# A two-layer gated-linear-attention decoder step on eight cores: 256-token pairs, one mixed last tile, cast weight loads during the other phase, sample states in phase 2, decay kept in the state

## The chip, the cores and the metric

One Trainium2 chip, all eight cores, one program on each: a core has one prompt sequence of 2048 positions and 16 sample sequences of 4 tokens, and no core talks to another. The metric is device time in microseconds (us) of the slowest core. Cores 0 to 3 are one die, 4 to 7 the other. In some executions the cores of one die show a lower granted TensorE clock and take some per cent longer (in one of before, 1661.4 us, cores 0 to 3 had a mean clock of 0.80 to 0.82 and took 1611 to 1660 us, cores 4 to 7 had 0.92 to 0.93 and took 1494 to 1519); such an execution is called slow, and only fast ones are compared.

## The reference

Each of two layers does this for every token (cut to what matters here; `gla_scan` is the recurrence over tokens, `pool_mix` trailing means over 2, 4, 8 and 16 positions):

```python
xn = rmsnorm(h, norm_g)
q, k, v, ga, u, gb, alow, mg = split(xn @ w_in)              # 6160 columns
la = log_sigmoid(alow @ w_alpha + b_alpha) / 16              # the decay, per key channel
o, S_new = gla_scan(q * 128 ** -0.5, k, v, la, S0)           # S = exp(la) S + k^T v ; o = q S
ya = (rmsnorm_per_head(o) * gla_gain * silu(ga)) @ w_a
yb = (pool_mix(u) * silu(gb)) @ w_b
h = h + (sigmoid(mg_a) * ya + sigmoid(mg_b) * yb) @ w_out
```

The prompt starts from an empty state after 16 learned meta tokens; each sample has its own state (4 heads x 128 x 256 f32, 512 KB), which goes in and comes out updated. Outputs are the final normalised rows, the states of prompt and samples, and the last 15 pooling inputs.

## The kernel before

A layer runs in two phases. Phase 1 makes q, k, v, gates, attention and pooling branch tile by tile (128 tokens) and parks its results in HBM; phase 2 reads them back for the merge gates and the output projections. One weight buffer in SBUF serves both phases. Layer 0's phase-1 weights are cast from f32 as they are loaded; the other three sets are first cast into bf16 copies in HBM, a few pieces per tile, and loaded from there when the buffer is free:

```python
def emit_stage(pieces, k):                 # during phase 1 and 2 of layer 0
    ...
    dma(o_, i_, r=[], w=["S" + sub], eng="pool", after=aft, max_dma_last_dim=4096)   # f32 -> bf16 copy in HBM
def load_w(l, ph, aft=None, only=None):
    if aft is None:
        aft = tuple(phase_pe_ops)          # the buffer is free when the other phase's matmuls are done
    ...
        dma(o_, so_, r=stage_keys.get(key, ["S" + key]), w=[key], after=aft, eng=STAGED_Q)
```

Tile 0 holds the samples and meta tokens, and in it the sixteen sample states pass through before the prompt starts:

```python
for s in range(NSS):                       # inside tile 0 of phase 1
    ld(s + NSL - 1)                                            # 512 KB in
    cp("act", S_bfs[i2][:, :], S_in[i3][:, :], ...)            # to bf16
    for h in range(4): mm(b_[0:n, off:off + 256], qm[i2]..., S_bfs[i2]..., ...)
    for hp in range(2): ...                                    # k^T v, and S = e S + that, on VectorE
    dma(nsg_s[l, s]..., S_in[i3]...)                           # 512 KB out
```

Sigmoids take three passes of ScalarE, with one load of a function table in the whole trace, and PSUM is handed out by the bank (the kernel allocates eight of 128 x 512 f32):

```python
act(egi, b_[:, 0:4 * n], AF.Exp, ..., scale=-1.0)
act(buf_ap, buf_ap, AF.Ln, ..., bias=1.0, scale=1.0)
act(buf_ap, buf_ap, AF.Exp, ..., scale=-1.0)
```

## Time and profile before

| | before |
|---|---|
| median of 4 runs | 1529.1 us (1523.0 to 1532.7) |
| profiled execution, slowest core (3) | 1523.1 us, cores 1500.4 to 1523.1 |
| bytes moved by DMA | 201.4 MB |
| TensorE work if each matmul started when it could | 1179 us |
| lost to the lowered clock after stops | 43 us |
| matmuls waiting, start included | 301 us |

The last three rows are worked out from the trace: the time from each matmul's start to the next is split into N/2.4 + 2.5 ns of work for N columns (a line through the medians of before at full clock, where matmuls of 80, 128, 256 and 512 columns start every 36, 56, 109 and 216 ns; 25 ns at least and twice the columns for f32), the excess while the recorded clock was below 1, and the rest. I call them work, cold and gaps. The page of before, busy time and then forty equal slices of the span (tenths of busy time for an engine, of full speed for the clock, of 16 engines for DMA):

```profile
PE 1277.0 (84%) x17416; PEld 1077.1 (71%) x17416; DVE 629.6 (41%) x1153; ACT 935.8 (61%) x2563; POOL 556.2 (37%) x838
...
PE   2446599999996699999965679999999839999998
...
PEclk9757799999998799999987599999999969999999
DMA  9999978759555787843246861111111192333321
```

The reader should see four dense stretches of PE at 9, and between them dips in which DMA is at 9 or the clock is low: start, change to phase 2, change of layer, second sample loop.

### The profile page before, as it was taken

How to read it: one execution, taken by the hardware profiler on the slowest of the kernel's cores; microseconds unless marked ns; L12 is line 12 of the kernel's file. 1: busy time of each engine (PE TensorE's matmuls, PEld its weight loads, DVE VectorE, ACT ScalarE, POOL GpSimd, SP SyncE). 2: the span in 40 equal slices, each digit the busy share in tenths (PEclk: the TensorE clock that was granted, in tenths of full speed). 3: DMA queues.
4: the chain of work that ended last, by engine and by line, in shares of the span. 5: the costliest groups of instructions: out<-in, count | busy, mean ns of one | idle time of the engine just before them, and what ended most of it. 6: DMA issues, size and time to landing. Idle time of an engine off the chain costs nothing.

```text
span 1523.1 us, 46175 instructions; the slowest of 8 cores (1500.4 to 1523.1 us)
## 1 busy us (share of the span) xinstructions
PE 1277.0 (84%) x17416; PEld 1077.1 (71%) x17416; DVE 629.6 (41%) x1153; ACT 935.8 (61%) x2563; POOL 556.2 (37%) x838
## 2 busy tenths in 40 slices
PE   2446599999996699999965679999999839999998
PEld 2225588888875588989843367888787739989886
DVE  2243255555544032232223545555555403333333
ACT  2225277777765276767732367777776708777776
POOL 0422366665555143322214334444344502222221
PEclk9757799999998799999987599999999969999999
DMA  9999978759555787843246861111111192333321
GB/s 182 216 240 189 171 116 144 139 82 144 107 83 132 239 160 188 172 136 117 92 142 198 280 194 52 54 63 58 64 59 37 66 286 79 109 109 107 119 95 70
DMA packets 108086, 201.41 MB, mean 132 GB/s; under 512 B 11674, under 2 KB 54426, under 8 KB 107064
## 3 DMA queue, kind: packets, MB, share of 16 engines
q1 hardware_dynamic: 80040, 134.72, 28.0%
q0 software_dynamic: 27824, 63.74, 25.0%
q8 instruction: 138, 2.26, 0.6%
q14 instruction: 84, 0.69, 0.2%
HBM read 176.94 MB, written 85.95 MB: 173 GB/s over the span
## 4 chain that ended last, share of the span: by engine, by line
PE 63%; DMA 15%; ACT 5%; issue 5%; DVE 5%; POOL 3%; SPq 3%; DVEq 0%; ACTq 0%; POOLq 0%
PE bank L467 61%; DMA sb_WB<-WS 7%; DMA sb_S_in_all<-sgla 3%; DMA sb_WB<-w_in 3%; SPq L526 3%; PE bank L474 2%; DVE sb_S_in_all L505 2%; ACT sb_v_tok L485 1%; DMA sb_hb<-xp 1%; ACT sb_tmpA L485 1%; DMA nsg_s<-sb_S_in_all 1%; POOL sb_kdT L493 1%; DVE sb_tmpB L712 1%; ACT sb_eg L485 1%; POOL sb_sB L493 1%
## 5 line engine op out<-in xcount | busy, mean ns | idle before, releaser
L467 PE MATMUL bank<-sb_xnT,sb_WB 128*128 128x128 bf16 (+3 forms) x11152 | 710.7, 222 | 89.9 <-DMA sb_WB<-WS 54.6
L467 PEld LDWEIGHTS bank<-sb_xnT,sb_WB 128*128 128x128 bf16 (+1 forms) x11152 | 651.1, 100 | 116.9 <-issue 53.3
L493 POOL TENSOR_TENSOR sb_mergedT<-sb_tbuf 128x128 bf16<-128x128 f32 (+1 forms) x272 | 121.6, 449 | 426.3 <-DVE sb_tbuf L493 361.3
L485 ACT ACTIVATE sb_e_0<-bank,sb_negc 128x128 f32<-128x128 f32 (+1 forms) x272 | 89.8, 358 | 128.8 <-PE bank L467 123.0
L467 PE MATMUL bank<-sb_oTg,sb_WB 128*128 128x128 bf16 (+1 forms) x2176 | 162.5, 219 | 4.2 <-DMA sb_WB<-WS 4.2
L493 DVE TENSOR_TENSOR sb_tbuf<-bank,sb_e_0 128x256 f32<-128x256 f32 (+1 forms) x136 | 56.8, 418 | 223.3 <-ACT sb_e_0 L485 217.4
L467 PE MATMUL bank<-sb_WB,sb_xnT 128*128 128x512 bf16 (+1 forms) x544 | 134.5, 389 | 5.8 <-DMA sb_WB<-w_in 4.7
L467 PEld LDWEIGHTS bank<-sb_oTg,sb_WB 128*128 128x128 bf16 x2176 | 131.2, 99 | 4.4 <-issue 4.4
L485 ACT ACTIVATE sb_e_1<-sb_e_1 128x256 f32<-128x256 f32 (+1 forms) x272 | 111.5, 410 | 21.0 <-ACT sb_e_1 L485 3.0
L467 PE MATMUL bank<-sb_WB,sb_mergedT 128*128 128x512 bf16 (+1 forms) x544 | 123.0, 379 | 0.5 <-POOL sb_mergedT L493 0.5
L485 ACT ACTIVATE sb_e_0<-sb_e_0 128x256 f32<-128x256 f32 (+1 forms) x272 | 111.4, 409 | 14.9
L493 DVE TENSOR_TENSOR sb_eg<-bank,sb_eg 128x512 f32<-128x512 f32 (+1 forms) x68 | 46.2, 680 | 150.7 <-POOL sb_eg L493 150.7
L493 DVE TENSOR_TENSOR sb_tbuf<-bank,sb_e_1 128x256 f32<-128x256 f32 (+1 forms) x136 | 56.6, 417 | 112.5 <-ACT sb_e_1 L485 85.3
L467 PE MATMUL bank<-sb_ypTg,sb_WB 128*128 128x128 bf16 (+1 forms) x1088 | 101.7, 218 | 0.3 <-DMA sb_WB<-WS 0.3
L493 POOL TENSOR_TENSOR sb_eg<-sb_eg,sb_cols 128x512 f32<-128x512 f32 (+1 forms) x68 | 69.4, 1021 | 81.3 <-ACT sb_eg L485 80.8
L485 ACT ACTIVATE sb_e_1<-bank,sb_negc 128x128 f32<-128x128 f32 (+1 forms) x272 | 91.7, 360 | 8.7 <-DVE sb_tbuf L493 2.7
L485 ACT ACTIVATE sb_S_bfs<-sb_S_in_all 128x1024 bf16<-128x1024 f32 x32 | 33.6, 1055 | 99.1 <-DMA sb_S_in_all<-sgla 96.0
L467 PEld LDWEIGHTS bank<-sb_WB,sb_mergedT 128*128 128x128 bf16 (+1 forms) x544 | 52.3, 99 | 57.0 <-issue 1.4
L467 PEld LDWEIGHTS bank<-sb_WB,sb_xnT 128*128 128x128 bf16 (+1 forms) x544 | 51.4, 102 | 57.8 <-DMA sb_WB<-w_in 5.0
L485 ACT ACTIVATE sb_xsb<-sb_hb 128x1024 bf16<-128x1024 f32 (+1 forms) x51 | 54.5, 1068 | 58.4 <-DVE sb_hb L493 36.5
L485 ACT ACTIVATE sb_eg<-sb_eg 128x512 f32<-128x512 f32 (+1 forms) x136 | 84.4, 622 | 5.7
L505 DVE SCALAR_TENSOR_TENSOR sb_S_in_all<-sb_S_in_all,sb_ebcm,bank 128x256 f32<-128x256 f32 x128 | 58.4, 478 | 57.7 <-ACT sb_S_bfs L485 47.1
(113 smaller groups left out, 1817.5 us busy)
## 6 DMA issues: line engine op xcount, KB each, us to landing
sb_WB<-WS POOLq DMA_DIRECT2D x12, 2048.0 KB, 23.4
sb_hb<-xp SPq DMA_DIRECT2D x32, 512.0 KB, 7.1
sb_S_in_all<-sgla SPq DMA_DIRECT2D x32, 512.0 KB, 6.9
nsg_s<-sb_S_in_all SPq DMA_DIRECT2D x32, 512.0 KB, 5.7
WS<-w_in POOLq DMA_DIRECT2D x64, 256.0 KB, 10.3
sb_hb<-H SPq DMA_DIRECT2D x32, 512.0 KB, 3.6
XN<-sb_xnT SPq DMA_DIRECT2D x34, 256.0 KB, 4.9
OT<-sb_oTg SPq DMA_DIRECT2D x34, 256.0 KB, 2.2
```

The lines of the kernel that those rows point to most:

```text
L467: i_ = S.add("pe", lambda e: e.matmul(out, lhsT=lhsT, rhs=rhs, start=start, stop=stop, skip_group_check=sgc), r=r, w=w, cost=c, lat=250.0, ...
L474: return S.add("pe", lambda e: e.transpose(out, in_, ident), r=r, w=w, cost=c, lat=250.0, attach=True)
L485: return S.add("act", lambda e: e.activation(out=out, in_=in_, func=func, **kw), r=r, w=w, cost=c, lat=120.0)
L493: return S.add(eng, lambda e: e.tensor_tensor(out=out, in0=in0, in1=in1, op=op), r=r, w=w, cost=ecost(eng, fsz(out)), lat=120.0)
L505: return S.add("dve", lambda e: e.scalar_tensor_tensor(out=out, in0=in0, scalar=scalar, in1=in1, op0=op0, op1=op1), r=r, w=w, cost=ecost(" ...
L526: return S.add(eng, lambda e: e.dma_start(out=out, in_=in_, **kw), r=r, w=w, dma=True, after=after, cost=nb / 300.0)
L712: S.add("dve", lambda e: e.tensor_tensor_scan(out=tmpB[:, 0:4 * n], data0=cf[:, rmc:rmc + 4 * n], data1=tmpA[:, 0:4 * n], initial=0.0, op0 ...
```

## The change

A rewrite of nearly the whole kernel. Its intent: wider tiles and fewer instructions, no weight wait at a change of phase, and no sample loop in phase 1's way. Prompt tokens go in pairs of 128-token tiles; the 64 sample tokens and the last 16 prompt tokens form one mixed tile of 80 at the end. Weights have three regions (one for phase 1, one for phase 2, one shared) and are cast straight from f32 while the other phase runs. Sample states are read and updated in phase 2, between merge blocks. The running state is kept undecayed, the decay multiplying it one tile later. Sigmoid becomes a tanh. PSUM is mostly taken in pairs of banks. The core of the diff, cut:

```diff
-    WS = {(0, 2): dscr("WS02", [128, WB_ELEMS], BF16), (1, 1): dscr("WS11", ...   # bf16 copies in HBM
-        def emit_stage(pieces, k): ...
-        def load_w(l, ph, aft=None, only=None): ...
+        def load_w1_v(l):                      # q, k, v, decay weights
+            for a, b in ((0, O_K), (O_K, O_V), (O_V, O_V + 4096), (O_V + 4096, N_V1)):
+                dma(V1[:, a:b], w1[l, :, a:b], eng="pool")           # f32 in HBM -> bf16 in SBUF
+        def load_w1_r(l): ...                  # gates, pooling: shared region, 4 transfers
+        def load_w2_v(l):                      # six of eight merge blocks
+            for c in range(N_EARLY_C):
+                dma(V2[:, c * CB:(c + 1) * CB], w2[l, :, c * CB:(c + 1) * CB], eng="pool")
+        def load_w2_r(l): ...                  # last two blocks, output matrix: shared region
 ...
-                act(egi, b_[:, 0:4 * n], AF.Exp, r=[bk_], w=["eg%d" % i], scale=-1.0)
-                sigmoid_inplace(egi, "eg%d" % i)
+            act(dst, bank(b_)[:, 0:4 * n], AF.Tanh, scale=0.5)
+            stt(dst, dst, 1.0, bank(b_)[:, 0:4 * n], ALU.add, ALU.mult)
+            banks.free(b_)                     # a pair of banks
 ...
-                    act(b..., AF.Exp ...); Ln; scan; Exp; Exp     # decay, 128 tokens
+            act(A, bank(b2)[:, 0:4 * n], AF.Exp, scale=-1.0)        # decay, 256 tokens
+            act(A, A, AF.Ln, bias=1.0, scale=1.0)
+            ... scan ...
+            act(A, B, AF.Exp, scale=-1.0 / 16.0)
+            act(B, B, AF.Exp, scale=1.0 / 16.0)
 ...
+        def phase1(l):
+            front(l, 0); decay(l, 0); front(l, 1)
+            for p in range(NPAIR):
+                q_, k_ = q_k(p)
+                v0 = v_proj(p, 0); decay(l, p + 1); v1 = v_proj(p, 1); k_tok(p, k_)
+                scores(p, 0, q_, k_); gate_a(l, p, 0); bo0 = attend(p, 0, q_, v0)
+                scores(p, 1, q_, k_); gate_a(l, p, 1); normalise(bo0, 128, on[0], 0)
+                bo1 = attend(p, 1, q_, v1); pool_u(l, p); normalise(bo1, 128, on[1], 1)
+                gate_b(l, p); gate_o(...); front(l, p + 2); pool_y(l, p); gate_o(...)
+                if p == 0:
+                    load_w2_v(l)
 ...
+        def phase2(l):                         # units: sample_read, sample_write, spread over the blocks
+            ...
+                    while done < len(units) and done * total < k * len(units):
+                        units[done]()
```

A list scheduler orders each engine's instructions after this; it moves loads up as soon as their destination is free in its own estimate. So layer 0's six `load_w2_v` transfers stand at the program's start, not after pair 0.

## The prediction

> **What bounds the kernel now.** I read the spans of the cores first (1500.4 to 1523.1 us, dies within 1% at one clock: undisturbed), then the chain of waits, then busy time by stage, then the groups by shape. The chain, on the page:
>
> ```profile
> PE 63%; DMA 15%; ACT 5%; issue 5%; DVE 5%; POOL 3%; SPq 3%; DVEq 0%; ACTq 0%; POOLq 0%
> ```
>
> Two thirds is TensorE; the next is transfers. The stages (start:end, length, busy us with instruction counts of PE, PEld, DVE, ACT, POOL, then granted clock, DMA share, GB/s) say where each sits:
>
> ```profile
> 18.00:165.00 147.00, 68.56 (x480) 45.73 (x478) 44.79 (x88) 43.06 (x98) 37.29 (x52) 0.71 0.96 206
> 165.00:490.00 325.00, 300.15 (x4141) 257.84 (x4138) 174.28 (x299) 232.01 (x599) 192.96 (x249) 0.98 0.72 121
> 490.00:524.00 34.00, 14.02 (x231) 13.63 (x232) 0.42 (x2) 2.19 (x10) 0.66 (x2) 0.64 0.91 301
> 524.00:780.00 256.00, 255.75 (x3840) 225.33 (x3838) 77.06 (x167) 180.77 (x536) 77.44 (x169) 1.00 0.55 134
> 816.00:900.00 84.00, 49.78 (x414) 31.35 (x412) 42.51 (x82) 32.69 (x74) 29.91 (x38) 0.72 0.82 254
> 900.00:1220.00 320.00, 300.42 (x4113) 253.00 (x4109) 175.66 (x300) 230.11 (x607) 142.43 (x170) 1.00 0.17 59
> 1256.00:1512.00 256.00, 255.53 (x3840) 225.36 (x3840) 94.70 (x182) 197.80 (x598) 60.92 (x136) 1.00 0.29 99
> ```
>
> The four dense stages (325, 256, 320, 256: 1157 us) are TensorE-bound: phase 2 without a gap, phase 1 with about 6% of gaps. The other 366 us are start (165), three changes of phase or layer (34, 36, 36), the second layer's sample loop (84) and tail (11): DMA 0.8 to 0.96 busy, a clock near 0.7, PE mostly waiting. What it waits for:
>
> ```profile
> PE bank L467 <- DMA sb_WB<-WS: 60.2, 11, 17.6
> PE bank L467 <- ACT sb_S_bfs L485: 43.9, 9, 11.2
> PE bank L467 <- DMA sb_WB<-w_in: 26.4, 3, 14.2
> ```
>
> These are weights that can be loaded only when one shared weight buffer is free, and sample states (512 KB in, cast, 512 KB out, sixteen per layer) that the first tile of phase 1 walks through before the pipeline starts.
>
> [...]a phase-2 tile is 224x55.8 + 16x215.8 = 15.95 us, and 16 tiles 255.2 us against 256 measured for 3840 matmuls. So weight loads are hidden even at 128 columns, and doubling the width wins 2%, not half.
> [...]1.00 granted through 256 us with all eight cores dense. I assume 1.00 after as well.
> [...]in the first 60 us the two queues take 51.7% and 44.1% of them, an even split.
>
> **The change part by part.**
> *Weights.* The cast copies of weights in HBM go (64+16+16+8 transfers of 256 KB, and reading them back); f32 weights are cast straight into three regions: one for phase 1 alone, one for phase 2 alone, one shared. From 120 to 170 us of before, the GpSimd queue moved 4.93 MB (counted at the bf16 end) in 76.4% of 16 engines' time: 129 GB/s of engine time; in the first 60 us, 147. I take 140, as rows are longer now (an estimate).
> The order of the built program shows two things that the diff does not. First, GpSimd issues fourteen weight transfers at the start; from the ninth on each waits for the completion of the one eight earlier (eight semaphores), and all fourteen stand ahead of the first norm's small GpSimd operations. So the first normalised tile waits until transfer six has landed: 24,704 elements x 128 x 2 B = 6.32 MB, at 140 GB/s 45 us, plus 6 us for about 2 MB of rows and pass-through on the other queue, plus 6 us of start, norm and transposes. **PE starts at about 57 us.** By then its weights are there (the last two land within 16 us more). Before spent 165 us here but did a tile and the sample loop in it.
> Second, at the end of layer 0 the six phase-2 blocks of layer 1 (5.5 MB) come free one by one in the mixed tile and enter the queue ahead of the gate weights that layer 1's first pair needs (two transfers, 2.1 MB). 7.6 MB at 140 GB/s is 54 us, with sharing and latency about 60 us from the mixed tile's beginning. PE has from there about 24 us of phase 2 and 19 us of q, k, v, decay before it needs them. **Stall about 15 us.**
> In the other direction, six of eight blocks are loaded early, so phase 2 starts at once; blocks 7 and 8 (needed 18 us later) make it, and the output matrix (needed after some 38 us, landing in 28 to 49) may cost 5 us.
>
> *Phase 1.* Per pair of 256 tokens: 204 matmuls of 256 columns (22.3 us), 32 of 512 (6.9), 48 of 128 (2.7; 32 in layer 1, whose transposed input is made in phase 2), 24 of 256 for attention and state (2.6), 8 f32 halves for the gate (2.0, from 288 ns each at 128 columns, mostly pipelined): 36.5 us, 35.6 in layer 1. Two tiles of before are 2x18.5 = 37.0 by the same count, but took 2x20.1. The recurrence (state matmul 0.44, four updates of 478 ns, four scaled casts on GpSimd near 450 ns) is 5 us per 128 tokens, far below 18. Sigmoid by tanh takes one ACT pass instead of three; ACT needs about 24 us a pair, DVE 26 (from 1225 ns per 1024-element evacuation, 690 per 512, 478 per update), POOL 16: all under 36. I leave 5% of gaps, less than before's 7.5%. With a mixed tile of 12.5 us (80 columns cost 35.8 ns): 8x36.5+12.5 = 304.5, **320** with gaps; layer 1 297.5, **312**.
>
> *Phase 2.* A pair is 224x109.2 + 32x215.8 = 31.4 us; layer 0 adds 0.9 for the next layer's transposes. Samples come on top: per state 8 matmuls of 4 columns (8 weight loads, about 0.5 us) and 4 of 256 (0.44): 16 us a layer, and 2 for the final f32 product. The mixed tile is 11.5. **288 and 281.** This is more than before's 256 plus its own first tile (16), but the 43 to 50 us of sample matmuls, and above all their waits, are gone from phase 1.[...]
>
> *Sum:* 57 + 320 + 11 (into phase 2, 6 of chain and 5 of output weights) + 288 + 15 + 312 + 8 + 281 + 8 (last norm and store) = **1300 us**. Against before by stage: start and first phase 490 to 377, second 290 to 299, layer 1's first 440 to 327, last 303 to 297. So nearly all the gain is stall taken out (about 230 us), hardly any is the wider matmul.
>
> **The rivals.**
> *The start stays long.* If casts run at the 105 GB/s seen when 4.2 MB took 40.6 us with other traffic (124 to 165 us), start is 75 us, the stall at layer 1 is 30, the output matrix is 15 late: 1350. For it: the DMA share is 0.96 there already. Against: no sample states compete now.
> *Phase 1 gets new gaps.* Tanh and Ln may need different function tables; the one load in this trace took 1283 ns, and two per pair would be 2.6 us of ACT; the fixed order of the list scheduler then makes PE wait, since each gate holds two of eight banks. For it: ACT was the busiest helper (230 of 320 us). Against: it has 12 us of slack per pair. At 12% of gaps instead of 5: +42 us, 1342.
> *Sample states disturb phase 2.* Each needs load, cast, update, store with three buffers; an in-order PE waits when a cast is late, mostly in the first 60 us beside the weight loads. One microsecond per state is +32 us. Against: 16 us per state is available.
> [...]
>
> **Range and chances.** These shift the sum by -20 to +50 each, rarely all together: 1255 to 1350. To end within 2% of 1532 it would have to lose 200 us more than I count, which no rival gives. Faster 0.97, same 0.02, slower 0.01.
>
> **What would show each step.** First matmul between 50 and 65 us, and released by the norm, behind a GpSimd wait on weight transfers; if PE begins by 30 us, the reading of the queue is wrong. Phase-1 pairs at 37 to 39 us, PE busy 95%; phase-2 pairs at 33 to 34 us (109 ns per 256-column matmul, clock 1.00); a single wait of 5 to 25 us for the gate weights soon after layer 1 begins, named as a DMA. No PE wait for sample states over 2 us. A granted clock below 0.95 in dense stages, or a GpSimd that is busy over 80% of phase 1, would make the prediction wrong.

Times of a matmul (35.8, 55.8, 109.2 and 215.8 ns at 80, 128, 256 and 512 columns) agree with the medians of before's trace at full clock, 36, 56, 109 and 216 ns. Two of 128 columns are thus 112 ns against 109 for one of 256, and in the phase-2 line at 524 PEld's 225.33 us lie beside a PE that is busy for 255.75 of 256. The 1.00 holds for all eight cores: each had four stretches of 266 us or more without a lower record. "Of them" means the time of 16 DMA engines; the 51.7% are those of GpSimd's queue, from which both kernels issue all casts. Two small times are estimates: 6 us for 2 MB on the other queue (that queue's 134.72 MB in 28.0% of the engines' span in before, 316 GB/s, would give 6.3), and 0.5 us for eight matmuls of 4 columns (not shown in before; in after they start every 25 ns). Cut with the rest are a fourth rival, faster casts at 1280 us, which is the -20 of the range, and the rate that was set against the 16 MB of state transfers (in after's phase 2 the DMA share is 0.52).

## The result

The changed kernel took 1427.5 us (median of 4 runs, 1426.2 to 1428.8), before 1529.1 us. A ratio is the mean time of one kernel's fast runs over that of the other's fast runs of the same rounds, so not quite the ratio of these medians: 0.9349, 95% interval 0.9322 to 0.9376. It is faster by 6.5%, where 15% was predicted, and outside the range. By the accounting above, on the slowest core (2, 1426.0 us): work 1157 us (predicted 1171), cold 34, gaps 235. Of the 97 us gained, 66 are gaps, 10 are cold and 21 are work. The same lines of the page, after:

```profile
PE 1234.5 (87%) x10600; PEld 944.4 (66%) x10600; DVE 627.4 (44%) x942; ACT 524.7 (37%) x1020; POOL 462.6 (32%) x810
...
PE   0369889998887789999996599999999899999997
...
PEclk9988999999998889999999699999999999999999
DMA  9992011111029975555349711100111594655421
```

PE starts late and has eights and sevens where 9 was expected, DMA is at 9 in the same three places as PE's dips, and ScalarE fell from 61% to 37%. Its chain of waits, summed by engine:

```profile
PE 68%; DMA 10%; DVE 8%; issue 5%; POOL 5%; ACT 3%; DVEq 0%; POOLq 0%; ACTq 0%; SPq 0%
```

TensorE's share rose by 5 points and DMA's fell by 5, but VectorE went from 5 to 8. The stages of after, with the columns that the prediction explains (start:end, length, busy us and counts of PE, PEld, DVE, ACT, POOL, clock, DMA share, GB/s):

```profile
0.00:56.00 56.00, 0.00 (x0) 0.00 (x0) 3.44 (x15) 3.58 (x5) 9.72 (x24) 1.00 0.97 166
56.00:132.00 76.00, 56.04 (x346) 39.14 (x347) 25.85 (x29) 26.05 (x48) 17.23 (x36) 0.87 0.75 153
132.00:445.00 313.00, 279.05 (x2450) 212.49 (x2447) 178.47 (x267) 147.64 (x271) 138.37 (x245) 0.99 0.20 64
445.00:517.00 72.00, 56.74 (x458) 44.84 (x456) 20.34 (x34) 16.64 (x35) 14.58 (x23) 0.85 0.92 204
517.00:757.00 240.00, 235.12 (x2156) 182.93 (x2156) 103.65 (x157) 76.44 (x168) 63.81 (x109) 1.00 0.52 165
757.00:835.00 78.00, 48.48 (x334) 33.12 (x333) 19.71 (x23) 23.12 (x41) 14.11 (x31) 0.78 0.72 130
835.00:1085.00 250.00, 232.60 (x1837) 174.88 (x1834) 127.03 (x184) 113.91 (x205) 99.50 (x169) 0.96 0.10 35
...
1131.00:1418.00 287.00, 284.55 (x2550) 223.60 (x2548) 118.88 (x191) 96.98 (x208) 82.33 (x143) 1.00 0.52 161
```

Phase 2 (fifth and last line) is dense, as predicted. The excess is in the first pair (76 us), in the pairs of phase 1 (third and seventh line), and at the two changes (72 and 78 us, 57 and 48 of them busy). What PE waited for over the whole span (us in total, times, longest):

```profile
PE psum L509 <- DVE arena L546: 66.9, 18, 56.2
PE psum L503 <- DVE arena L551: 54.3, 38, 5.5
PE psum L503 <- ACT arena L530: 34.3, 5, 18.4
...
PE psum L503 <- DMA arena<-YP: 6.9, 1, 6.9
```

The first is the start, 56.2 us. The second is waits for the VectorE update that frees a gate's banks; 40.6 us of it lie in the pairs of phase 1. The third has one wait of 18.4 us at the change of layer. No wait for gate weights is on the list, though one was predicted. The start on GpSimd (start, length, instruction, idle time before it and what ended that):

```profile
1.54 4.50 POOL L571 DMA_DIRECT2D arena<-w  x8 [0.84 <-POOLq L356]
...
16.11 0.54 POOL L571 DMA_DIRECT2D arena<-w  x1 [9.91 <-DMA arena<-w]
...
53.25 0.53 POOL L571 DMA_DIRECT2D arena<-w  x1 [5.49 <-DMA arena<-w]
...
54.64 0.57 POOL L538 TENSOR_TENSOR arena<-arena 128x1 f32<-128x1 f32 x1 [0.21 <-POOL arena L546]
```

Eight weight transfers go out at once; six more wait for landings; the norm's power runs at 54.64 and PE begins at 56.2. That is the predicted start to the microsecond. The long pieces of DMA in the chain of waits after the start (start, length, transfer):

```profile
87.87 12.72 DMA arena<-hin
...
448.78 39.71 DMA nsg_p<-arena
...
488.63 13.61 DMA arena<-sgla
...
759.24 13.82 DMA XN<-arena
...
774.21 18.90 DMA XN<-arena
```

None of these is a weight. They are four tiles of 512 KB, which land in 3 to 6 us (median) over the whole run, and one of 160 KB (the last), and here take 13 to 40 while casts are under way (small_rows tests the link): from 56 to 110 us the cast queue took 78% of the engines' time, from 735 to 835 us 62% against 10% for the other queue. And a pair of phase 1 around PE's stop:

```profile
939.60 1.28 ACT L530 ACT_TABLE_LOAD   x1 [1.29 <-PE psum L503]
940.72 0.87 DVE L551 SCALAR_TENSOR_TENSOR arena<-arena,psum 128x256 f32<-128x256 f32 x2 [1.70 <-PE psum L503]
940.90 1.02 ACT L530 ACTIVATE arena<-psum 128x1024 f32<-128x1024 f32 x1
...
942.03 2.00 DVE L551 SCALAR_TENSOR_TENSOR arena<-arena,psum 128x1024 f32<-128x1024 f32 x3 [0.44 <-ACT arena L530]
...
943.31 0.94 PE L503 MATMUL psum<-arena 128*128 128x256 bf16 x7 [2.03 <-DVE arena L551]
```

The gate's matmuls are done at 939.6; table load, tanh and update follow in a row, the update frees the banks, and PE starts again after 2.03 us. In each of the six steady pairs of layer 1 a window of 3.4 us at half clock follows, 1.7 us of cold by the accounting. By core the same run has one to six such windows: the stage takes 247.8 us on cores with one and 249.8 on this one, so a window costs 0.4 us there; the rest of the 1.7 comes back as shorter waits (gaps of 31.5 us with one window, 25.2 with six). The function table is loaded 32 times in the run (1283 ns each, 41.1 us of ScalarE), once in before. In this pair one load stands before the decay's logarithm (934.13) and one before the gate's tanh (939.60); with an exponential in the logarithm's place (no_ln, below) one load is left in the whole run. So a decay and a gate cost a load each.

### The profile page after: what moved, and what is told of

Read it like the earlier page. It is cut to its first block, busy times and chain, and to the rows that moved or that the text cites. A ratio compares the mean times of both kernels' runs of the same rounds, so it can differ in the third digit from the quotient of the medians.

```text
span 1426.0 us, 28355 instructions; the slowest of 8 cores (1417.4 to 1426.0 us)
## 1 busy us (share of the span) xinstructions
PE 1234.5 (87%) x10600; PEld 944.4 (66%) x10600; DVE 627.4 (44%) x942; ACT 524.7 (37%) x1020; POOL 462.6 (32%) x810
## 4 chain that ended last, share of the span: by engine, by line
PE 68%; DMA 10%; DVE 8%; issue 5%; POOL 5%; ACT 3%; DVEq 0%; POOLq 0%; ACTq 0%; SPq 0%
PE psum L503 65%; DVE arena L551 6%; DMA arena<-w 3%; ACT arena L530 3%; DMA nsg_p<-arena 3%; DMA XN<-arena 2%; POOL arena L546 2%; PE psum L509 2%; POOL arena L538 2%; DVE arena L546 1%; DMA arena<-sgla 1%; DVE arena L538 1%; DMA arena<-hin 1%; POOL arena L571 1%; DVE arena L697 0%
## 5 line engine op out<-in xcount | busy, mean ns | idle before, releaser
L503 PE MATMUL psum<-arena 128*128 128x256 bf16 (+6 forms) x9888 | 1195.0, 282 | 113.9 <-DVE arena L551 54.3
L503 PEld LDWEIGHTS psum<-arena 128*128 128x128 bf16 (+2 forms) x9888 | 901.3, 101 | 391.3 <-ACT arena L530 67.3
L551 DVE SCALAR_TENSOR_TENSOR arena<-arena,psum 128x256 f32<-128x256 f32 (+4 forms) x454 | 258.5, 607 | 226.5 <-PE psum L503 197.2
L538 POOL TENSOR_TENSOR arena<-arena 128x256 bf16<-128x256 f32 (+13 forms) x321 | 265.7, 832 | 280.6 <-DVE arena L551 227.9
L530 ACT ACTIVATE arena<-psum 128x256 bf16<-128x256 f32 (+9 forms) x308 | 199.4, 660 | 370.0 <-PE psum L503 341.3
L546 POOL TENSOR_SCALAR arena<-arena 128x256 f32<-128x256 f32 (+5 forms) x389 | 165.2, 436 | 495.4 <-PE psum L503 263.4
L530 ACT ACTIVATE arena<-psum,arena 128x256 f32<-128x256 f32 (+2 forms) x356 | 145.5, 456 | 303.5 <-PE psum L503 215.6
L530 ACT ACTIVATE arena<-arena 128x1024 bf16<-128x1024 f32 (+2 forms) x137 | 138.6, 1028 | 186.6 <-DVE arena L551 134.5
L538 DVE TENSOR_TENSOR arena<-psum,arena 128x1024 bf16<-128x1024 bf16 (+4 forms) x120 | 124.4, 1038 | 168.4 <-PE psum L503 128.2
L551 DVE SCALAR_TENSOR_TENSOR arena<-psum,arena 128x256 bf16<-128x256 f32 (+4 forms) x124 | 91.3, 764 | 90.2 <-PE psum L503 86.9
L509 PE MATMUL psum<-arena 128*128 128x128 bf16 (+4 forms) x712 | 54.1, 226 | 69.4 <-DVE arena L546 66.9
L546 DVE TENSOR_SCALAR arena<-arena 128x1024 bf16<-128x1024 f32 (+4 forms) x45 | 29.4, 662 | 122.5 <-POOL arena L538 103.1
L546 DVE TENSOR_SCALAR arena<-psum,arena 128x256 bf16<-128x256 f32 (+1 forms) x68 | 29.8, 479 | 111.7 <-POOL arena L538 100.6
L530 ACT ACT_TABLE_LOAD x32 | 41.1, 1283 | 35.6 <-PE psum L503 18.5
L571 POOL DMA_DIRECT2D arena<-w x36 | 20.4, 575 | 60.1 <-DMA arena<-w 44.4
```

The lines of the kernel that those rows point to most:

```text
L503: return S.add("pe", lambda e: e.matmul(out, lhsT=lhsT, rhs=rhs, start=start, stop=stop, skip_group_check=sgc), r=[lhsT, rhs], w=[out], co ...
L509: return S.add("pe", lambda e: e.transpose(out, in_, ident), r=[in_, ident], w=[out], cost=c, lat=250.0, attach=True)
L530: return S.add("act", lambda e: e.activation(out=out, in_=in_, func=func, **kw), r=r, w=w, cost=c, lat=150.0)
L538: return S.add(eng, lambda e: e.tensor_tensor(out=out, in0=in0, in1=in1, op=op), r=[in0, in1], w=[out], cost=ecost(eng, fsz(out)), lat=120.0)
L546: return S.add(eng, lambda e: e.tensor_scalar(out=out, in0=in0, **kw), r=r, w=[out], cost=ecost(eng, fsz(out), 0.6), lat=120.0)
L551: return S.add("dve", lambda e: e.scalar_tensor_tensor(out=out, in0=in0, scalar=scalar, in1=in1, op0=op0, op1=op1), r=r, w=[out], cost=eco ...
```

## The experiments

Fifteen kernels ran, with three timed rounds each. To compare stages, I use that every kernel has 10,600 weight loads: a stage ends where the same weight load by number starts (where an edit reorders matmuls within a pair, the edge is off by a few us). Lengths in us, on one core without a long stretch at a clock of 0.8125 (see own_xno for that). It is the slowest such core, but core 6 of 6 and 7 in gate_half and core 5, the shortest of six, in own_xno_hold_l1; there the text gives the others too.

| stage | after | hold_l0 | gate_half | own_xno | own_xno_hold_l1 | best_a | best_b | best_d |
|---|---|---|---|---|---|---|---|---|
| to first matmul | 56.2 | 36.0 | 55.2 | 56.0 | 55.3 | 21.1 | 25.4 | 20.4 |
| first pair, layer 0 | 76.2 | 68.7 | 74.9 | 76.8 | 73.5 | 83.7 | 70.7 | 74.2 |
| pairs 2 to 8 | 312.9 | 318.5 | 287.8 | 310.7 | 311.1 | 293.9 | 286.8 | 294.5 |
| mixed tile, into phase 2 | 72.3 | 72.6 | 74.7 | 70.3 | 69.4 | 69.7 | 59.6 | 59.0 |
| phase 2, layer 0 | 239.9 | 239.9 | 240.2 | 239.4 | 238.4 | 255.1 | 252.6 | 245.5 |
| into layer 1 | 77.7 | 75.3 | 91.4 | 67.5 | 52.7 | 53.9 | 55.7 | 55.6 |
| pairs, layer 1 | 249.8 | 249.7 | 233.3 | 254.6 | 265.0 | 254.7 | 241.7 | 237.9 |
| mixed tile, layer 1 | 45.9 | 45.8 | 43.9 | 47.4 | 47.4 | 43.9 | 43.9 | 43.9 |
| phase 2, layer 1, tail | 295.3 | 295.5 | 295.0 | 294.6 | 294.8 | 293.8 | 302.3 | 306.5 |
| span of that core | 1426.0 | 1402.0 | 1396.2 | 1417.5 | 1407.5 | 1369.8 | 1338.6 | 1337.4 |

**My theory** was that the missing 130 us have three sources: GpSimd blocked at the start, table loads in phase 1, and casts that take the engines from the tiles beside them. Rivals are named with each run.

### hold_l0: layer 0's phase-2 blocks after the first pair

```diff
             for c in range(N_EARLY_C):
-                dma(V2[...], w2[...], eng="pool")
+                i = dma(V2[...], w2[...], eng="pool"); l in (0,) and hold(S, i)
 ...
+def hold(S, i): ...          # after scheduling, move it behind the last operation emitted before it
```

> Only edit: the six phase-2 weight blocks of layer 0 are issued after the first pair instead of at the program's start; every other engine's order is the same. Theory (the start is lost twice: GpSimd is blocked on semaphores behind the casts, and casts take the transfer engines from the input rows): first matmul at 20 to 25 us instead of 56, end of the first pair at 90 to 95 us instead of 133, whole time 1427 - 40 = 1387 us (1375 to 1395). Rival (the first pair is bound by the landing of its own eight weight transfers, 8.4 MB at 155 GB/s = 54 us, and its casts compete anyway): the first matmul comes early but the pair still ends near 115 to 125 us, whole time 1410 to 1420.

The profiled execution was fast, 1403.5 us; the three timed ones were slow (1499 to 1508), so there is no interval, but their undisturbed dies had spans of 1391 to 1417. Start and first pair together fell from 132.3 to 104.7 us. The first matmul was at 36.0 us on the slowest core and at 19.2 to 36.0 on the eight, not at 20 to 25: GpSimd's block was gone and something else stood behind it, as the chain shows:

```profile
2.84 36.39 DMA arena<-hin
```

The first two input tiles, 512 KB each, took 28.9 and 36.4 us to land beside eight casts. So the block was real, worth 20 us of start. The 28 us with the pair aren't its alone, since the edit also takes six casts away from the first pair; pairs 2 to 8, where they now run, took 6 us longer.

### hin_first: input before casts

```diff
-                    dma(h, hin[r0:r0 + n, :])
+                    j = dma(h, hin[r0:r0 + n, :]); t == 1 and [S.ops[w]["deps"].update({j: "RAW"}) for w in S.w1]
```

(with hold_l0's edit; `S.w1` are the eight phase-1 casts.)

> Edit: as in hold_l0, and the eight phase-1 weight casts of layer 0 are issued only when the first two input tiles have landed (in hold_l0 the first tile of 512 KB took 36.4 us to land beside them, as the chain of waits shows). The scheduler moves some of the first pair's work. Theory (casts starve the input rows at the start): the two tiles land by 8 to 10 us, first matmul at 11 to 16 us, the first pair ends at 82 to 92 us instead of 104.7 in hold_l0 and 132.3 in the changed kernel, fast time 1376 to 1390 us (hold_l0's profiled fast run: 1403.5). Rival (casts bound it: 8.4 MB at 155 GB/s is 54 us, now starting 7 us later): first matmul early, but the pair ends at 100 to 112 us, fast time 1400 to 1412.

First matmul at 12.2 to 12.8 us on all cores, as expected. But the first pair ended at 110.7 us on core 4 (span 1402.6, no lowered clock), within the rival's 100 to 112: PE waited 21.5 us in one piece for weights, which had all landed only at 75.7 us. From 13.4 us that is 8.6 MB in 62 us, 138 GB/s. So the start is bound by the casts themselves once nothing else is in the way; 105 us, hold_l0's, was what could be had here by ordering. The median time was 1428.2 us (ratio 0.9371, interval 0.9352 to 0.9390), though the four cores without a lowered clock took 1403 to 1410 us; on the other four it was lowered, see own_xno.

### small_rows: casts in pieces of 1 KB

```diff
-                dma(V1[:, a:b], w1[l, :, a:b], eng="pool")
+                dma(V1[:, a:b], w1[l, :, a:b], eng="pool", max_dma_last_dim=2304)     # so for all four loads
```

> Only edit: the casting weight transfers are cut into pieces of 512 to 576 elements (about 1 KB at the bf16 end instead of 7 to 8 KB); orders stay the same. Theory ([...]the queue with packets of 700 ns against 136 to 256 ns gets 80 to 90% of them): beside casts an input tile of 512 KB lands in 5 to 9 us instead of 15 to 17, the store of the last mixed tile in 5 to 8 instead of 14 to 19, the prompt state's store in under 15 instead of 40; the other queue's share in the first 56 us rises from 11% to over 25%. The casts themselves land later in the same measure, so the first matmul stays at 56 to 65 us; whole time 1385 to 1415 us. Rival (the casts win by their rate or by arriving first, not by packet length): landings and shares within 15% of before, time 1420 to 1432 us.

("Of them" means the engines' time, of which the cast queue had 86.7% in the first 60 us of after.)

1471.4 us, ratio 0.9663 (0.9625 to 0.9701): 3% slower than after. In the first 60 us cast packets had a mean of 1016 B and 121 ns instead of 7427 B and 777 ns. What the other queue's tiles took to land in the first 60 us, after first and then this run (issues, KB each, median us):

```profile
arena<-hin SPq DMA_DIRECT2D x4, 512.0 KB, 17.4
```

```profile
arena<-hin SPq DMA_DIRECT2D x2, 512.0 KB, 9.8
```

The landing nearly halved (the first two tiles: 13.6 and 20.9 us, then 8.3 and 11.3), and the first pair fell from 76.2 to 63.4 us. The store of the prompt's state at the change to phase 2, after first and then this run:

```profile
nsg_p<-arena SPq DMA_DIRECT2D x1, 512.0 KB, 39.7
```

```profile
nsg_p<-arena SPq DMA_DIRECT2D x1, 512.0 KB, 10.8
```

The store of the last mixed tile fell from 18.9 to 6.7 us. So the landings did what the theory of packet length said; the other queue's share at the start did not (13% after 11%, over 25% expected). In time nothing came of that: neither the change of phase nor that of layer got shorter, and the first matmul came at 84.8 us:

```profile
1.57 2.90 POOL L571 DMA_DIRECT2D arena<-w  x3 [0.88 <-POOLq L356]
22.50 0.89 POOL L571 DMA_DIRECT2D arena<-w  x1 [18.03 <-issue]
```

After three transfers GpSimd stood for 18 us with nothing to wait for but its own issue, and 4 to 7 us before each further one. Three transfers of 128 rows in 8 pieces are 192 pieces an engine, if they spread evenly over 16 (an estimate); what GpSimd stood for isn't shown. Everything behind on GpSimd waited, at the start and in phase 2 of both layers (15 and 9 us longer). So the cut pays at one place and costs at another; a longer piece had to be tried (best_b).

### tanh_early, no_ln, tanh_early2: the table load

tanh_early put a one-column tanh after the decay's last exponential:

```diff
-            act(B, B, AF.Exp, scale=1.0 / 16.0)
+            ... e.activation(out=b, in_=b, func=AF.Exp, scale=1.0 / 16.0); e.activation(out=j, in_=j, func=AF.Tanh)
```

> Only edit: right after the last exponential of each decay a one-column tanh is issued on ScalarE, so that the table load for tanh comes there, while PE has work, and not between the gate's matmuls and its tanh. Results stay correct; the number of table loads stays about 32. Theory (each pair loses 1.28 us at the gate to the table load, and the stop of over 2 us brings one 3.4 us window of half clock, 1.7 us lost): phase-1 pairs of layer 1 go from 41.1 to about 38.3 us, the half-clock windows vanish there, whole time down by 16 x 2.8 = 45, say 35 to 50: 1377 to 1392 us. Rival (the stop is set by banks and by the DVE update after the tanh, and the clock window by something else): pairs stay above 40.3 us, whole time 1415 to 1427.

1430.6 us, ratio 0.9399 (0.9341 to 0.9456): no change, and no test either. The timeline shows that the scheduler puts the exponentials after the gate's tanh, so in most pairs the load stayed where it was. The second try put it after the logarithm; the run without a logarithm (wrong result, relative error 0.91) takes both loads away:

```diff
-            act(A, A, AF.Ln, bias=1.0, scale=1.0)
+            act(A, A, AF.Exp, bias=1.0, scale=-1.0)          # no_ln
```

> Wrong result on purpose: the logarithm of the decay is replaced by an exponential of the same shape, so that ScalarE needs one table only; every engine's order is the same. Theory of the table load: loads fall from 32 to 1 or 2, and the time is that of the early tanh within 8 us (1375 to 1395 us), as only the load at the gate is on PE's path, not the one at the logarithm. Rival A (the load at the logarithm costs too): 1350 to 1370, another 16 x 1.3 us less than the early tanh. Rival B (loads don't matter): 1420 or more.

> The changed kernel with one edit: a one-column tanh right after the logarithm of each decay, so that tanh's table load comes there and not at the gate (the first try put it after the exponentials, which run after the gate's tanh, so it changed nothing). Results correct, 32 to 36 loads. If the load at the gate is what the run without logarithm removed: like that run, pairs of layer 1 at 40.1 to 40.5 us instead of 41.0, no half-clock windows there, 1410 to 1418 us. If the load matters in full (1.28 us and 1.7 us of clock a pair): 1385 to 1395. If not at all: 1422 to 1430.

no_ln: one load, 1414.5 us, ratio 0.9290 (0.9256 to 0.9324). tanh_early2: 1418.8 us, 0.9304 (0.9288 to 0.9320). Both shortened the pairs of layer 1 from 249.8 to 243.8 us and had no half-clock window there. So in the pairs only the load at the gate mattered, not the one at the logarithm, and it was worth 9 us of the whole, not 45. What PE waited for in those pairs, after first, then no_ln:

```profile
PE psum L503 <- DVE arena L551: 17.2, 12, 2.0
```

```profile
PE psum L503 <- DVE arena L551: 13.1, 11, 1.5
PE psum L503 <- DVE arena L546: 8.9, 6, 1.5
```

The stop at the gate went from 2.0 to 1.5 us, and a second stop of 1.5 us, for the normalise (L546), came in behind it. In after the half clock had hidden it: core 7, with one window, has it too (7.7 us in 5 waits), core 2, with six, hasn't. More waiting in sum than on this core before, and no cold, but the 6 us aren't all the clock's: the cores of after with one window instead of six are 2.0 us shorter, so six windows account for some 2.4 us (an estimate from that) and the load for the rest. My theory of the load fell: it is one link of a row.

### gate_half: gate projections in single banks

```diff
-            b_ = banks.pair()
-            for c4 in range(4): proj(...)
-            act(dst, ..., AF.Tanh, scale=0.5); stt(dst, ...); banks.free(b_)
+            for k in range(2):
+                b_ = banks.one()
+                for c2 in range(2): proj(...)
+                d_ = dst[:, 2 * k * n:2 * (k + 1) * n]; act(d_, ..., AF.Tanh, scale=0.5)
+                stt(d_, ...); banks.free(b_)
```

> Edit: the two output-gate projections of a pair use four single PSUM banks instead of two pairs of banks, with a tanh and an update of 512 columns for each bank; the scheduler moves other instructions a little. Theory (PE stops about 2.2 us in each pair for a pair of banks that waits for table load, tanh and update in a row; halving pipelines this): phase-1 pairs of layer 1 go from 41.0 to 38 to 39.5 us, eight half-clock windows there mostly vanish, whole time down by 25 to 45 us: 1382 to 1402. Rival (the stop only moves to the next wait, the normalise, as in the run without the logarithm where 6 us per layer came back): pairs at 40 to 40.5, whole time 1410 to 1420.

Median 1427.5 us, ratio 0.9335 (0.9287 to 0.9384), but one of its runs took 1409.3, and cores 6 and 7 of the profile, the only ones without a lowered clock, 1396.2 and 1404.8. On core 6 the pairs of layer 0 fell by 25.1 us, those of layer 1 by 16.5, to 38.2 us each, with no half-clock windows in the steady pairs; table loads stayed. Of PE's waits in layer 1 the gate's nearly went:

```profile
PE psum L503 <- DVE arena L546: 10.4, 6, 1.8
PE psum L503 <- DVE arena L551: 2.1, 7, 0.8
```

What had been missed is the row "load, tanh, update, banks free" of 3.7 us behind a pair of banks, while PE had 1.7 us of other work; in halves the load runs under the second half's matmuls (on core 6 a load at 922.89 us, while PE runs from 920.21 on for 13.71 us). Core 7 agrees (288.0 and 233.2 us for the pairs). Into layer 1 took 13.7 us longer on core 6 and 18.3 on core 7. There PE, earlier than in after, now waited for weights, for which it waits nowhere in after:

```profile
PE psum L503 <- DMA arena<-w: 27.4, 2, 14.0
```

The two waits end as the gates' first transfer and the one after the gates land. This is the predicted stall, behind the six blocks, and larger than predicted.

### own_xno, own_xno_hold_l1: the change of layer

```diff
-        xnO = new_bf(2048)                                   # in bytes that the decay's buffer uses in phase 1
+        ... xnO = new_bf(2048) as the last of phase 2's region
```

> Edit: phase 2's outgoing normalised tile no longer shares bytes with the gate buffer of the next layer's decay (it moves to the end of phase 2's region), so layer 1's decay needn't wait for its store; the scheduler moves work at the change of layer, and one wait of VectorE on itself is made explicit. Theory of the prediction (the gate weights of layer 1, queued behind 5.5 MB of phase-2 weights, are the next limit, landing near 812 us): the 18.5 us stop vanishes but a wait for weights of 8 to 15 us appears, stage into layer 1 goes from 77.7 to 66 to 73 us, whole time 1415 to 1422. Rival (weights are early enough): stage 55 to 60 us, whole time 1405 to 1410.

> Edit: as in own_xno, and the six early phase-2 blocks of layer 1 are issued after that layer's first pair, so the gate weights go ahead of them; only GpSimd's queue differs from own_xno. Theory of the prediction (the blocks ahead of the gate weights cost a stall): stage into layer 1 falls to 48 to 55 us against own_xno's 66 to 73, whole time 1395 to 1405. Rival (no stall from the queue): same as own_xno within 4 us.

own_xno, core 2: into layer 1 67.5 us, from 77.7, and 13.2 us of waits for weights in place of the 18.4 us behind ScalarE:

```profile
PE psum L503 <- DMA arena<-w: 13.2, 2, 8.5
```

This is the predicted stall of 15 us (8.5 for the gates' first transfer, 4.7 for the one after the gates). In after it was there, covered by a longer wait: the decay's exponential could not overwrite bytes of the outgoing tile until its store had landed, 18.9 us beside casts. With the six blocks behind the gate weights (own_xno_hold_l1, core 5) the stage took 52.7 us and no weight was waited for, but the pairs after it took 10 us longer than in own_xno, 8.1 of them one wait:

```profile
PE psum L503 <- DMA arena<-XN: 8.1, 1, 8.1
```

The casts, moved, now ran beside that pair's input tile. On the six cores with a full clock the stage took 53 to 56 us and the pairs after it 265 to 268, where after has 75 to 78 and 248 to 250: nearly all of the gain was given back.

In time neither was faster than after: 1433.7 (0.9408, 0.9393 to 0.9423) and 1433.4 us (0.9389, 0.9350 to 0.9428). The other part of the reason is in the clock of single cores. Phase 2 of layer 0, own_xno, on core 0 and on core 2, same columns:

```profile
513.00:640.00 127.00, 126.34 (x950) 95.52 (x954) 49.89 (x76) 35.57 (x72) 28.23 (x46) 0.83 0.49 170
```

```profile
513.00:640.00 127.00, 125.42 (x1107) 99.06 (x1106) 55.62 (x85) 40.79 (x83) 31.80 (x51) 1.00 0.56 192
```

Both are busy throughout; core 0 got 0.83 of the clock and did 950 matmuls against 1107. The records show 0.8125 for 100 to 160 us, from the change into phase 2 on, on cores 0, 1, 4 and 5, and in three kernels (hin_first, gate_half, own_xno_hold_l1) on two to six cores too (in gate_half in phase 1 as well), each time on two neighbours together. In after and before no core had such a record.

### after_again: the control

> The changed kernel unedited, as a control: in the last four runs, on another chip, several cores were granted 0.8125 of the clock for 100 to 160 us from the change to phase 2 of layer 0 on, and their spans were 15 to 30 us longer than those of cores that weren't. Theory A (it belongs to the chip): on such a chip the control shows the same windows and 1440 to 1450 us. Theory B (it belongs to the edits, which make that stretch denser): the control has no windows over 10 us and 1424 to 1431 us.

1425.3 us, ratio 0.9360 (0.9319 to 0.9401), profiled run without any 0.8125 record. But this ran on a third chip, and the three kernels with it had none longer than 15.1 us either. So theory B's numbers came, and still it can't be said whether chip or edit brought the lowered clock: that stays open. The edits alone don't: best_a has three of the four kernels' edits and its longest record is 15.0 us, and one execution of gate_half in the call with the lowered clock (1409.3 us) had all eight cores at a mean of 0.96 or more. What stands is what the cores with a full clock show, in one execution each: gate_half 1396 and 1405 us, hin_first 1403 to 1410, own_xno 1412 to 1418, own_xno_hold_l1 1408 to 1420, against 1417 to 1426 in after; and that a slowest-core time can be 15 to 30 us longer than they are.

### best_a, best_b: all together, and with longer short pieces

```diff
+ hold for layers 0 and 1; gate_half; xnO of its own                                   # best_a
-                    if l + 1 < NL: load_w1_v(l + 1)          # at the end of phase 2, hoisted to its start
+                if p == 3 and l + 1 < NL: load_w1_v(l + 1)   # held there
+ max_dma_last_dim=4608 on every cast: 4 pieces a row, about 2 KB                      # best_b adds this
```

> Combination, results correct: early phase-2 blocks held behind the first pair in both layers, gate projections in single banks, the outgoing tile in bytes of its own, and layer 1's q, k, v weights cast only from the middle of layer 0's phase 2 on. If the terms add up on a core without lowered clock: start and first pair 133 to 105, pairs of both layers minus 42, into layer 1 78 to 53 with 8 given back by a late input tile, into phase 2 of layer 0 72 to 65: about 1325 to 1345 us; with lowered clock up to 25 more. Rival (the gains overlap, and each wait removed uncovers the next): 1365 to 1390.

> As best_a, with all casts in rows of 896 to 1152 elements (about 2 KB at the bf16 end, 4 pieces a row), so that input tiles beside them land sooner while GpSimd isn't held up[...] as with 1 KB rows. Theory (a landing beside casts is set by the length of the cast packets): first input tile in 8 to 20 us instead of 36, start to end of first pair 85 to 98 us instead of 105, the late input tile of layer 1 gone: 1305 to 1330 us, 12 to 25 below best_a. Rival (landing gains are paid by later weights and blocked GpSimd issues): within 8 us of best_a.

best_a: 1371.4 us, ratio 0.9002 (0.8968 to 0.9035), in the rival's range: the gains overlap. best_b: 1340.1 us, 0.8801 (0.8766 to 0.8835), 31 us less. It differs from best_a in nothing but the length of the cast pieces, so these 31 us are the packet length's, 23 of them in two stages. best_a and then best_b, input tile of layer 1:

```profile
PE psum L503 <- DMA arena<-XN: 20.3, 1, 20.3
```

```profile
PE psum L503 <- DMA arena<-XN: 7.5, 1, 7.5
```

and into phase 2, 69.7 to 59.6 us. In after's stretches with casts the cast queue's packets took 650 to 780 ns and the other's 130 to 175 (means), and the cast queue had 58 to 87% of the engines' time, the other 10 to 31%; how an engine chooses between its queues isn't shown. A rival is untested: shorter pieces also make GpSimd stand, which spaces the casts out, and no run parts the two. Not all of the expectation came: the first matmul was at 25.4 us, since GpSimd stood 15 us before the eighth transfer (7 x 32 = 224 pieces an engine had gone, by the same count), and phase 2 of layer 1 took 8 us longer on this core (1 to 13 on the eight), 4.3 of them a wait for weights.

best_b beats both kernels: by its ratio over the control's (0.8801/0.9360) it is 6.0% faster than the changed kernel, and 12% faster than before. Its results are correct.

### best_c, best_d, best_e: what is left

```diff
-                ts("pool", dst[...], ..., colsh[:, c:c + 1], ...)
+                ts(("pool", "dve")[r], ...)                   # best_c: half of the gain on VectorE; else best_a
+ casts two at a time in pairs 1 to 3; layer 1's q, k, v in four pairs of phase 2      # best_d; else best_b
+ the gain's 16 operations emitted after the normalise's                               # best_e; else best_d
```

> As best_a, with the gain of the second half of the gate applied on VectorE instead of GpSimd. With single banks the pair still stopped 1.8 us for the normalise, whose two small GpSimd operations stood behind 13 scaling operations (5.85 us). Theory (that queue sets the last stop): the stop vanishes, pairs of layer 1 go from 38.3 to 36.5 to 37.3 us, 16 to 25 us below best_a. Rival (VectorE's longer queue takes its place): within 6 us of best_a or slower.

> As best_b, but casts spread: the six early phase-2 blocks two at a time in pairs 1 to 3 of each layer, right after the decay that used the newest input tile; layer 1's q, k, v weights one transfer in each of four phase-2 pairs; the first and last phase-1 piece in fewer, longer rows[...]. If the remaining waits come from casts beside tiles: first matmul at 13 to 18 us instead of 25, input wait of layer 1 (7.5 us) under 2, phase 2 of layer 0 at 242 to 246 instead of 252.6: 1312 to 1325 us. Rival (the casts' volume costs the same wherever it stands): 1333 to 1345.

> As best_d, with the gate's gain scaling (16 GpSimd operations a pair) emitted after the normalise's small operations instead of before, so that these don't stand behind 13 of them. If GpSimd's queue sets the last stop of a pair (1.9 us): pairs of layer 1 from 38.3 to 36.5 to 37.3 us, 16 to 28 us below best_d. If another wait takes its place: within 6 us of best_d.

best_c had two fast runs, 1383.7 and 1383.3 us, 12 slower than best_a, two slow ones, and no interval; PE's waits for the normalise grew from 8.6 to 12.5 us in layer 1. best_d: 1340.7 us, 0.8797 (0.8780 to 0.8814), the same as best_b. Each part did its work (first matmul 20.4, no input wait in layer 1, phase 2 of layer 0 7 us shorter) and was given back elsewhere: pairs 2 to 8 of layer 0 took 8 us longer, phase 2 of layer 1 4. The number is the rival's, that the volume of casts costs about the same wherever it stands; that it is the volume isn't shown. best_e: 1344.2 us, 0.8812 (0.8797 to 0.8827); the normalise waits stayed (10.8 us for 9.8). So GpSimd's order isn't the last stop's cause, or not alone; what is stays open.

## Why the prediction was right or wrong

Right: the mechanism of the gain, the work (1171 predicted, 1157 measured), the start (57 and 56.2, by the predicted block: transfer six landed at 52.7 us, some 51 estimated), phase 2 nearly (33 to 34 us a pair predicted, 34.6 to 35.1 measured), the full clock (1.00 in both phase 2), and that states in phase 2 cost little. Its sums hold to rounding, but before's pairs (2x20.1 for 2x18.5) have 8% of gaps, not 7.5, and the change of layer (780 to 816 us of before) has DMA at 0.66, not 0.8 to 0.96. Wrong: the sum of waits, 129 predicted, 269 measured; best_b has 181. By its own terms (cold and gaps, us, core 2 of after):

| term of the sum | predicted | measured | what the runs showed |
|---|---|---|---|
| start | 57 | 56.2 | hold_l0: the block was worth 20 |
| first pair, as 5% | 2 | 36.7 | input tiles beside casts; with tiles first, 8.6 MB of casts bind; at best 95 us together with the start (best_d) instead of 132 |
| other pairs of layer 0, 5% | 13 | 49.3 | gate_half takes 25 of it |
| into phase 2 | 11 | 21.2 | best_b: 13 less, 10 of it by packet length |
| phase 2, layer 0 | 0 | 9.5 | not resolved; casts put there add 6 to 15 |
| into layer 1 | 17 | 39.2 | own_xno and hold: 20 to 25 less, nearly all given back in the pairs |
| phase 1, layer 1, 5% | 13 | 41.1 | gate_half takes 18 of it |
| phase 2, layer 1, and tail | 16 | 15.0 | |

- **"Under 36 ... I leave 5% of gaps, less than before's 7.5%"** is the step that failed most. Phase-1 pairs took 41.0 to 42.5 us instead of 37 to 39. It compared busy time per engine with the pair's length, and ScalarE's 12 us of slack was real. But a stop is set by the row behind one pair of banks, not by the average. The rival "new gaps" named the table load and the held banks and priced them at 42 us; with 12% it was the better estimate. The load alone was worth 9 us; the pair of banks, with load, tanh and update in a row, 43 (14 to 18 of it given back at the change of layer, where PE then waits for weights).
- **"By then its weights are there"** held: the eight transfers of phase 1 had landed by 68.0 us, as estimated, and PE waits for none in the first pair. What failed is taking the pair as steady from there (2 us lost, 36.7 measured): its input tiles run beside six more casts, until 108.2 us, and took 12.7 to 17.4 us to land.
- **"An even split"** is the assumption under that. In before's first 60 us the queues shared about evenly (51.7% and 44.1%), with packets of 1343 and 1923 B. The prediction saw that rows would be longer and used it only to raise the cast rate (140 GB/s; 153 measured in the first 60 us). It missed what longer packets would do to the other queue: in after the cast queue took 86.7% there and the other 11.3%, and tiles of 512 KB took 13 to 40 us to land at the start and at both changes, against medians of 3 to 6. (Before's five input tiles took 11 to 19 us there too, but that queue moved 7.45 MB beside them, after's 2.06.)
- **The stall of 15 us at layer 1** was right in cause and nearly in size (13.2 in own_xno, 27.4 in gate_half) but not what bounded in after: the reuse of the outgoing tile's bytes, which the order of the program showed, came later and covered it.
- **"No PE wait for sample states over 2 us"** failed once: 8.3 us up to 503.4 us, the first state beside casts.

What remains open: whether chip or edit lowered the clock to 0.8125, what sets the last 1.8 us of a phase-1 pair, the 9.5 us in phase 2 of layer 0, and how much of best_b's gain is the packets' length by itself and how much the spacing of casts.

## What to carry to other kernels

When the input of a transfer is cut into longer rows, ask what runs beside it on the other queue: 2 KB pieces instead of 7 KB ones gave 31 us here at the same bytes, while 1 KB pieces, tried in the order of after, held up the issuing engine and cost 44. When a helper engine looks idle enough, look for the longest row of steps behind one PSUM allocation and compare it with the matmuls that stand between it and its next user; halving the allocation took 43 us out of the pairs of layers 0 and 1 with no work removed, though 14 to 18 came back as the next wait. And treat each removed wait as uncovering the next: the predicted stall was there, beneath a longer one.

## What the runs showed of the hardware

- A landing beside casts: at the start, beside cast packets of 777 ns (7.4 KB), a 512 KB tile took 13 to 36 us to land, beside ones of 121 ns (1 KB) 8 to 11, and 3 to 6 as the median of the whole run.
- GpSimd's issues, counted in pieces an engine as above: it stood 18 us after 192 (small_rows), 15 us after 224 (best_b), and not at all with 224 in eight transfers (best_d).
- The rate of casts: 134 to 161 GB/s of the engines' time in the changed kernels, counted at the bf16 end, little changed by the piece (whole runs: 134 at 1.0 KB, 149 at 1.9 KB, 156 at 6.9 KB).
- The clock in dense stretches: before and after ran 240 to 256 us dense on all eight cores at 1.00; 0.8125 was granted for 100 to 160 us in four kernels, to pairs of neighbouring cores (0, 1, 6 and 7 in one of them), not die by die. In a slow execution of before (1661.4 us) all four cores of a die have a mean of 0.80 to 0.82.
- The clock after stops: a stop of 2.0 us in each of six pairs brought a window of 3.4 us at half clock in one to six of them, by core, and stops of 1.5 us none; the price was 0.4 us of time a window.
- A table load: 1283 ns in each of 32. At 939.60 the tanh began 1.30 us after its load did, and so did the operation behind the load at 934.13, which had come 0.08 us after the end of another.
